# A layer kernel with RG-LRU and RWKV-7 heads: the substitution in the diagonal blocks moved from VectorE to GpSimd

## The chip, the cores and the metric

The kernel runs on one core of one Trainium2 chip. The core has five engines that run their own instruction queues in order and wait for each other by semaphores: PE (TensorE, matrix products), DVE (VectorE), ACT (ScalarE), POOL (GpSimd) and SP (SyncE, which issues the DMAs here). The metric is the device time of one execution in microseconds; lower is better.

## The reference, cut to what matters

The reference is one decoder layer in float32 over 512 tokens of 2048 features: an adaLN-modulated mixing sub-layer whose heads are half RG-LRU and half RWKV-7, then a SwiGLU sub-layer and a final norm. The change concerns the recurrence of the RWKV-7 heads (16 heads of 64 features):

```python
def step(state, inp):
    r_t, d_t, k_t, v_t, kk_t, a_t = inp
    sa = jnp.einsum('bhvk,bhk->bhv', state, -kk_t)
    state = (state * d_t[:, :, None, :]
             + sa[..., None] * (kk_t * a_t)[:, :, None, :]
             + v_t[..., None] * k_t[:, :, None, :])
    y_t = jnp.einsum('bhvk,bhk->bhv', state, r_t)
    return state, y_t
...
_, y = lax.scan(step, s0, xs)
```

## The kernel before

Large products are done as three float32r products of operands that are split exactly in two: `load_split` (L112) loads a weight tile of 128x512, ACT writes its high part (`whi`, L105) and DVE the rest (`wlo`, L106), and `mm3` (L122) issues `hi*hi`, `lo*hi` and `hi*lo` at L124, L125 and L126. Three buffers hold such split tiles.

The RWKV heads are worked in 8 pairs of heads, the 512 tokens in 8 chunks of 64. Within a chunk the recurrence is a triangular system, so each chunk needs the inverse of a 64x64 unit triangular matrix for each head. `rwkv_half` (L596) prepares four chunks of a pair (a "half"): among others the products `ps_gr` of L633, their masked copy `rw_gb` (L635) and, packed from its diagonal 32-blocks, `rw_dg` (L637, L639). It ends with `inverse` (L750 on), which is called 16 times, once for each half of each pair:

- L757, DVE: a 32x32 transpose spreads the diagonal blocks, one to a partition, as `rw_at`; L760 sets `rw_x` to the identity.
- L764 and L766: the forward substitution. 31 steps, each a product of two operands into `rw_xp` and an addition to `rw_x`, every one of them needing the one before; an instruction covers all 128 partitions and from 4 to 46 elements of each.
- L768 and L771, DVE: two transposes give the inverted blocks as `rw_xn` and `rw_xs`. L775, POOL: four copies into `bd_xt`.
- L783 and L793, PE: the lower left blocks from `rw_xn` and `rw_xs`; then the chain of the pair's state (`rwkv_chain`, L666) may use the half.

`rwkv_weave` runs five streams of such steps side by side: the chains, the first halves, the second halves, `rwkv_main` (what a pair needs of all tokens), and columns of the adaLN modulation (L199, `adaq`). Where none of them can go on, `weave` (L145) takes a step of the filler: the input projections, the RG-LRU heads (whose `lru_gates` has a one-column memset on POOL at L885, read by DVE at L887), and half of the output projection. `weave` decides by planned latencies, for an inverse `INVLAT = 30.2` us, in which order the steps are written. From that, the scheduler of the framework makes the order of each engine's queue, and inserts the semaphores. On POOL stand, beside the copies of L775, two copies for each half (L616, `bd_a`) and one memset for each pair (L554).

Of the kernel before, what the change touches and what calls it, by code (L numbers as in the profile page):

```python
# [8 lines left out]
F32 = mybir.dt.float32  # L9
# [3 lines left out]
ALU = mybir.AluOpType  # L13
AX = mybir.AxisListType
PSUM = bass.MemoryType.PSUM
DRAM = bass.MemoryType.DRAM

P = 128
S = 512
# [7 lines left out]
C = 64  # L27
# [6 lines left out]
# latencies (us) that weave() goes by when it orders steps; they bear on the order only  # L34
HOP = 1.10                      # a small product, its copy out of PSUM
LM1, LM2, LM3 = 4.2, 6.8, 9.0   # the steps of rwkv_main
LH0 = 4.8                       # rwkv_half's operands
INVLAT = 30.2                   # substitution in the diagonal blocks
LSN = 1.79                      # the next state
MODLAT = (4.0, 3.8, 2.0)        # a quarter of a column of mod, by kind  # L40

# columns of the packed per-feature vectors (one column holds 128 features)
# [14 lines left out]
# columns of the constants (shapes alone)  # L57
# [29 lines left out]
class Layer:  # L87
# [24 lines left out]
    def load_split(self, src, n):  # L112
        """src: DRAM [128, n] -> (hi, lo) float32r tiles [128, n]"""
        raw = self.wp.tile([P, self.wc], F32, tag="raw", name="wraw", bufs=self.wb[0])
        self.nc.sync.dma_start(out=raw[:, :n], in_=src)
        hi = self.wp.tile([P, self.wc], F32R, tag="whi", name="whi", bufs=self.wb[1])
        lo = self.wp.tile([P, self.wc], F32R, tag="wlo", name="wlo", bufs=self.wb[1])
        with self.tc.high_priority():
            self.split_into(hi[:, :n], lo[:, :n], raw[:, :n])
        return hi, lo  # L120
# [7 lines left out]
    def gemm_steps(self, ps, src, acts):  # L128
        """ps[128, S] = W^T acts, src: DRAM [128, nk * 128], acts: list of (hi, lo); yields after each k"""
        nk = len(acts)  # L130
        kp = self.wc // P
        for k0 in range(0, nk, kp):
            kn = min(kp, nk - k0)
            hi, lo = self.load_split(src[:, k0 * P:(k0 + kn) * P], kn * P)
            for k in range(kn):
                sl = slice(k * P, (k + 1) * P)
                self.mm3(ps, (hi[:, sl], lo[:, sl]), acts[k0 + k], k0 + k == 0, k0 + k == nk - 1)
                yield
# [6 lines left out]
    def weave(self, streams, filler):  # L145
        """Traces the next step of the first stream that can run, a step of filler when none can.
        A stream yields (its last step's us on the tensor engine, the us until the next can run,
        what must hold in the trace before that); filler yields None or such a condition."""
        t = 0.0
        live = [[g, 0.0, None] for g in streams]  # L150
        fcond = None
        while live:
            for st in live:
                if st[1] <= t and (st[2] is None or st[2]()):
                    try:
                        with self.tc.issue_after(self.pe):
                            dur, lat, st[2] = next(st[0])
                        t += dur
                        st[1] = t + lat
                    except StopIteration:  # L160
                        live.remove(st)
                    break
            else:
                if filler is not None and (fcond is None or fcond()):
                    try:
                        fcond = next(filler)
                        t += 0.65
                    except StopIteration:
                        filler = None
                else:  # L170
                    t = min(st[1] for st in live if st[2] is None or st[2]())

# [1 line left out]
    def mod_pair(self, j):  # L174
        """columns j and j + 16"""
        nc = self.nc
        part = self.small.tile([P, 2], F32, tag="adapart", name="adapart", bufs=2)
        for h in range(2):
            t = self.ada.tile([P, D], F32, tag="ada", name="ada", bufs=4)
            nc.sync.dma_start(out=t, in_=self.i["w_ada"][j + 16 * h])  # L180
            nc.vector.scalar_tensor_tensor(out=t, in0=t, scalar=1.0, in1=self.cbc, op0=ALU.mult,
                                           op1=ALU.mult, accum_out=part[:, h:h + 1])
        o = _VOFF["b_ada"] + j
        nc.vector.tensor_tensor(out=self.mod[:, j:j + 17:16], in0=part, in1=self.vecs[:, o:o + 17:16],
                                op=ALU.add)

    def mod_steps(self, js, pool, tags):
        """the same for many columns, a quarter of c at a time"""
# [22 lines left out]
    def mod_scale(self, col, sc, g):  # L211
        """col = g * (1 + mod[:, sc])"""
        self.nc.vector.scalar_tensor_tensor(
            out=col, in0=self.mod[:, sc:sc + 1], scalar=1.0, in1=g, op0=ALU.add, op1=ALU.mult)

    def square(self, acc, x, k, pool):
        """acc += x * x"""
        if k == 0:
            self.nc.scalar.activation(out=acc, in_=x, func=AF.Square)
        else:  # L220
            t = pool.tile([P, S], F32, tag="ft", name="sqt", bufs=2)
            self.nc.scalar.activation(out=t, in_=x, func=AF.Square)
            self.nc.vector.tensor_tensor(out=acc, in0=acc, in1=t, op=ALU.add)

    def norm(self, acc, tag):
        """1 / rms of each token, in all partitions (PSUM), from sums of squares by partition"""
# [16 lines left out]
    def modulate(self, x, col, rstd, sh, lo=None):  # L243
        """hi, lo of x * col * rstd + sh"""
# [54 lines left out]
    def mixing(self):  # L299
# [3 lines left out]
        with ExitStack() as ctx:  # L303
            self.open_ada(ctx)
            with tc.tile_pool(name="xs", bufs=1) as xs:
# [16 lines left out]
                # seven tiles stay in PSUM, four more take turns in the last bank by quarters of K  # L322
# [43 lines left out]
    def rwkv_weave(self, kvr0, kvr1, u0):  # L366
# [16 lines left out]
        def filler():  # L383
# [15 lines left out]
            # half of the channels through the output projection  # L399
# [45 lines left out]
    def project(self, ys, half, *tags):  # L445
        """x1 += g_m * (ys through their half of w_out)"""
# [29 lines left out]
    def rwkv_setup(self, ctx):  # L476
# [4 lines left out]
        # zero at the first token of each chunk  # L481
# [3 lines left out]
        # block-diagonal operands (two heads); what lies off the blocks stays zero  # L485
# [7 lines left out]
    def lora_act(self, m, ps, pool):  # L493
        """what the second products of the low ranks take, the parts of a float32 stacked by rows:
        tanh(w) (hi, lo), a (lo, hi), all of g's first 128 rows, the other 32 (-, hi, lo, hi)"""
# [26 lines left out]
    def rwkv_main(self, pr):  # L522
        """what a pair of heads needs of all the tokens"""
# [16 lines left out]
        # decay and its running product within a chunk  # L540
# [21 lines left out]
        # kk = k * k_k over its norm per head  # L562
# [15 lines left out]
        # k' = k (1 + (a - 1) k_a), the bonus, v by tokens  # L578
# [17 lines left out]
    def rwkv_half(self, pr, hf):  # L596
        """four chunks of a pair"""
# [21 lines left out]
        # v by tokens, centred over its features  # L619
# [9 lines left out]
        # products within the chunks  # L629
# [36 lines left out]
    def rwkv_chain(self, pr):  # L666
        """a pair's state through the chunks, its output"""
# [9 lines left out]
        # through the chunks  # L677
# [49 lines left out]
        # group norm (y is centred already), bonus, gate  # L727
# [22 lines left out]
    def inverse(self, hf, dg, gb):  # L750
        """bd["xt"][hf]: the transposed inverse of I - A of each head and chunk, A^T in gb[:, :, :C]"""
# [3 lines left out]
        # diagonal 32-blocks, one to a partition (eight partitions share its columns)  # L755
# [6 lines left out]
        for s in range(31):  # L762
            n, j = 31 - s, s // 8 + 1
            tt(out=pr[:, :n, :j], in0=at[:, s + 1:, s:s + 1].to_broadcast([P, n, j]),  # L764
               in1=x[:, s:s + 1, :j].to_broadcast([P, n, j]), op=ALU.mult)
            tt(out=x[:, s + 1:, :j], in0=x[:, s + 1:, :j], in1=pr[:, :n, :j], op=ALU.add)  # L766
        xn = rw.tile([P, 32, 4], F32, tag=f"at{hf}", name="rw_xn")      # [t, j, chunk]
        nc.vector.transpose(out=xn.rearrange("p (j r) c -> p j (r c)", r=8),  # L768
                            in_=x.rearrange("p t j -> p j t"))
        xs = rw.tile([P, 4, 32], F32, tag=f"dg{hf}", name="rw_xs")      # [j, chunk, t]  # L770
# [7 lines left out]
        # lower left blocks: X21 = X22 A21 X11  # L778
# [22 lines left out]
    def lru_setup(self, ctx):  # L801
# [3 lines left out]
        # softplus(-lam) = max(-lam, 0) + 2 atanh(e / (2 + e)), e = exp(-|lam|)  # L805
# [24 lines left out]
    def lru_conv(self, j, pss=None):  # L830
        """head j: convolution"""
# [23 lines left out]
    def lru_gates(self, j):  # L855
        """gates, scan"""
# [18 lines left out]
        for m in range(2):  # L875
# [6 lines left out]
            # 1 - a^2 = tanh(-log a) (1 + a^2)  # L882
# [7 lines left out]
    def lru_gelu(self, j, pool, tags):  # L890
        """head j: its gelu branch"""
# [8 lines left out]
    def lru_out(self, j):  # L900
        """head j's product"""
# [78 lines left out]
def _tiles(w, mt=None):  # L980
    """[K, M] -> [M / 128, 128, K]: column tile m, partition p (row k * 128 + p), free (k, column)"""
# [4 lines left out]
def _pack(inp):  # L986
# [17 lines left out]
    lw = np.stack([a["lru_wa"][0], a["lru_wx"][0]], axis=1)          # [4, 2, 256, 256]  # L1004
# [41 lines left out]
```

## Time and profile before

| | |
|---|---|
| time, median of 3 runs | 2511.34 us (2509.75 to 2511.64) |
| the profiled execution: span from first to last instruction | 2515.8 us; the page gives no other time of it |
| busy: PE, DVE, ACT, POOL | 96%, 55%, 34%, 3% of the span |
| the weave of the RWKV heads | about 200 to 930 us of the span |
| L764 and L766 | 496 instructions each, 224.4 to 881.7 us |

The page's slices show in which part DVE is loaded; each digit is the busy share of a fortieth of the span (63 us) in tenths, PEclk the clock that PE was granted.

```profile
PE   5999999999999999899999999999999999999997
DVE  7979898999969847854423322233322233222244
POOL 0000111111101000000000000000000000000000
PEclk9999998999999999999999999999999999999998
```

DVE is near 9 tenths from the fourth to the fourteenth slice, which is the weave, and at 2 to 4 tenths in the SwiGLU part behind it. The first number behind a group in the tables of groups is its busy time in us, the second the mean time of one instruction in ns, and what follows the bar is the idle time of the engine ahead of it.

### The profile page before, as it was taken

What the parts mean: (1) busy time and instruction counts of PE and PEld (TensorE: products, weight loads), DVE (VectorE), ACT (ScalarE), POOL (GpSimd) and SP (SyncE); (2) the same over time, 40 slices, a digit from 0 to 9 for tenths busy, and PEclk for the clock granted to TensorE, in tenths of its full rate; (3) what the DMA queues carried; (4) which work ended last, traced back from release to release, by engine and by line L of the source; (5) the groups of instructions that cost most, each with busy time, mean ns of one, the idle gap of its engine ahead of it and who ended that gap; (6) DMA issues with size and microseconds to landing.
All of it is one profiled execution on the core that took longest, in us unless ns stands there. A gap on an engine that the chain in (4) does not pass through costs nothing.

```text
span 2515.8 us, 30983 instructions
## 1 busy us (share of the span) xinstructions
PE 2413.9 (96%) x11560; PEld 1953.4 (78%) x11560; DVE 1380.4 (55%) x3111; ACT 843.7 (34%) x1340; POOL 82.0 (3%) x131
## 2 busy tenths in 40 slices
PE   5999999999999999899999999999999999999997
PEld 3677777877777886687788888888888888888885
DVE  7979898999969847854423322233322233222244
ACT  4357364455355333432222222222222222222221
POOL 0000111111101000000000000000000000000000
PEclk9999998999999999999999999999999999999998
DMA  8864444444342438366423332323333233333233
GB/s 304 308 219 130 148 128 143 131 152 144 125 135 81 143 108 283 119 195 194 160 90 95 108 100 93 101 83 98 106 98 99 89 92 105 101 93 100 85 95 112
DMA packets 138938, 333.22 MB, mean 132 GB/s; under 512 B 15458, under 2 KB 28898, under 8 KB 134690
## 3 DMA queue, kind: packets, MB, share of 16 engines
q1 hardware_dynamic: 138788, 331.25, 40.7%
q8 instruction: 90, 1.47, 0.2%
q14 instruction: 60, 0.49, 0.1%
HBM read 322.92 MB, written 7.87 MB: 131 GB/s over the span
## 4 chain that ended last, share of the span: by engine, by line
PE 72%; DVE 9%; DMA 7%; issue 1%; ACT 1%; SPq 0%; POOL 0%; DVEq 0%; ACTq 0%
PE ps_mm L124 10%; PE ps_mm L126 10%; PE ps_mm L125 10%; PE ps_gr L126 6%; PE ps_st L124 6%; PE ps_gr L124 6%; PE ps_st L126 6%; PE ps_gr L125 6%; PE ps_st L125 6%; DMA adaq<-in_w_ada 6%; DVE adaq L199 2%; DVE wlo L106 2%; DVE rw_xp L764 1%; DVE rw_x L766 1%; DMA wraw<-in_w_out 1%
## 5 line engine op out<-in xcount | busy, mean ns | idle before, releaser
L106 DVE TENSOR_TENSOR wlo<-wraw,whi 128x1024 fp32r<-128x1024 f32 (+2 forms) x552 | 496.7, 902 | 730.2 <-ACT whi L105 721.1
L105 ACT CAST whi<-wraw 128x1024 fp32r<-128x1024 f32 (+2 forms) x552 | 436.6, 792 | 1292.4 <-PE ps_mm L125 401.1
L124 PE MATMUL ps_mm<-hhi,whi 128*128 128x512 f32 x1020 | 417.1, 410 | 9.8 <-ACT hhi L251 7.2
L126 PE MATMUL ps_mm<-hhi,wlo 128*128 128x512 f32 x1020 | 407.2, 399 | 1.7 <-DVE wlo L106 1.6
L125 PE MATMUL ps_mm<-hlo,whi 128*128 128x512 f32 x1020 | 406.5, 399 | 0.8 <-DVE hlo L252 0.7
L124 PEld LDWEIGHTS ps_mm<-hhi,whi 128*128 128x128 f32 x1020 | 193.4, 190 | 53.2 <-ACT hhi L251 9.9
L125 PEld LDWEIGHTS ps_mm<-hlo,whi 128*128 128x128 f32 x1020 | 193.7, 190 | 43.4 <-DVE hlo L252 4.8
L126 PEld LDWEIGHTS ps_mm<-hhi,wlo 128*128 128x128 f32 x1020 | 193.8, 190 | 42.3 <-DVE wlo L106 3.0
L199 DVE SCALAR_TENSOR_TENSOR adaq<-adaq,cbq 128x512 f32<-128x512 f32 x256 | 173.5, 687 | 92.9 <-DMA adaq<-in_w_ada 85.1
L126 PE MATMUL ps_gr<-hhi,wlo 128*128 128x512 f32 x496 | 193.7, 390 | 3.1 <-DVE wlo L106 3.1
L126 PE MATMUL ps_st<-hhi,wlo 128*128 128x512 f32 x496 | 193.6, 390 | 2.0 <-DVE wlo L106 2.0
L124 PE MATMUL ps_st<-hhi,whi 128*128 128x512 f32 x496 | 194.0, 391 | 1.6 <-ACT hhi L251 1.6
L125 PE MATMUL ps_gr<-hlo,whi 128*128 128x512 f32 x496 | 193.5, 390 | 0.0
L125 PE MATMUL ps_st<-hlo,whi 128*128 128x512 f32 x496 | 193.5, 390 | 0.0
L124 PE MATMUL ps_gr<-hhi,whi 128*128 128x512 f32 x496 | 192.6, 391 | 0.0
L126 PEld LDWEIGHTS ps_gr<-hhi,wlo 128*128 128x128 f32 x496 | 93.4, 188 | 23.6 <-DVE wlo L106 4.1
L126 PEld LDWEIGHTS ps_st<-hhi,wlo 128*128 128x128 f32 x496 | 93.4, 188 | 21.8 <-DVE wlo L106 2.5
L124 PEld LDWEIGHTS ps_st<-hhi,whi 128*128 128x128 f32 x496 | 93.5, 188 | 21.6 <-ACT hhi L251 2.2
L125 PEld LDWEIGHTS ps_gr<-hlo,whi 128*128 128x128 f32 x496 | 93.7, 189 | 19.6
L124 PEld LDWEIGHTS ps_gr<-hhi,whi 128*128 128x128 f32 x496 | 93.7, 189 | 19.4
L125 PEld LDWEIGHTS ps_st<-hlo,whi 128*128 128x128 f32 x496 | 93.3, 188 | 19.8 <-DVE hlo L252 0.3
L766 DVE TENSOR_TENSOR rw_x<-rw_x,rw_xp 128x27 f32<-128x27 f32 (+23 forms) x496 | 94.7, 196 | 5.7
(312 smaller groups left out, 3809.6 us busy)
## 6 DMA issues: line engine op xcount, KB each, us to landing
wraw<-in_w_gu SPq DMA_DIRECT2D x176, 512.0 KB, 3.6
adaq<-in_w_ada SPq DMA_DIRECT2D x256, 256.0 KB, 3.3
wraw<-in_w_in SPq DMA_DIRECT2D x160, 256.0 KB, 3.0
ada<-in_w_ada SPq DMA_DIRECT2D x32, 1024.0 KB, 7.2
wraw<-in_w_down SPq DMA_DIRECT2D x64, 512.0 KB, 3.5
wraw<-in_w_out SPq DMA_DIRECT2D x64, 256.0 KB, 3.3
wraw<-in_w_down SPq DMA_DIRECT2D x64, 192.0 KB, 2.3
x<-in_x SPq DMA_DIRECT2D x32, 256.0 KB, 5.3
```

The costliest lines, as they stand in the source:

```text
L105: nc.scalar.copy(out=hi, in_=src)
L106: nc.vector.tensor_tensor(out=lo, in0=src, in1=hi.bitcast(F32), op=ALU.subtract)
L124: mm(ps, lhsT=w[0], rhs=x[0], start=start, stop=False)
L125: mm(ps, lhsT=w[0], rhs=x[1], start=False, stop=False)
L126: self.pe = mm(ps, lhsT=w[1], rhs=x[0], start=False, stop=stop).ins
L199: nc.vector.scalar_tensor_tensor(out=t, in0=t, scalar=1.0, in1=cb, op0=ALU.mult, op1=ALU.mult, accum_out=part[:, m, h:h + 1])
L764: tt(out=pr[:, :n, :j], in0=at[:, s + 1:, s:s + 1].to_broadcast([P, n, j]), in1=x[:, s:s + 1, :j].to_broadcast([P, n, j]), op=ALU.mult)
L766: tt(out=x[:, s + 1:, :j], in0=x[:, s + 1:, :j], in1=pr[:, :n, :j], op=ALU.add)
```

## The change

The two instructions of each substitution step are issued on GpSimd instead of VectorE, in all 16 calls of `inverse`. Comments are emptied as well, line for line; the one added line shifts what stands behind it by one: L757, L764, L766, L768, L771, L775, L783, L793, L885, L887 are L758, L765, L767, L769, L772, L776, L784, L794, L886, L888 afterwards. The planned latencies stay as they are.

```diff
@@ -748,11 +748,12 @@
     def inverse(self, hf, dg, gb):
...
         nc, rw = self.nc, self.rw
         mm = nc.tensor.matmul
         tt = nc.vector.tensor_tensor
-        # diagonal 32-blocks, one to a partition (eight partitions share its columns)
+        gt = nc.gpsimd.tensor_tensor
+
         at = rw.tile([P, 32, 32], F32, tag=f"at{hf}", name="rw_at")
@@ -761,13 +762,13 @@
         pr = rw.tile([P, 31, 4], F32, tag=f"dg{hf}", name="rw_xp")
         for s in range(31):
             n, j = 31 - s, s // 8 + 1
-            tt(out=pr[:, :n, :j], in0=at[:, s + 1:, s:s + 1].to_broadcast([P, n, j]),
+            gt(out=pr[:, :n, :j], in0=at[:, s + 1:, s:s + 1].to_broadcast([P, n, j]),
                in1=x[:, s:s + 1, :j].to_broadcast([P, n, j]), op=ALU.mult)
-            tt(out=x[:, s + 1:, :j], in0=x[:, s + 1:, :j], in1=pr[:, :n, :j], op=ALU.add)
+            gt(out=x[:, s + 1:, :j], in0=x[:, s + 1:, :j], in1=pr[:, :n, :j], op=ALU.add)
```

The orders of the queues change with it. POOL's queue before, from the memset of the second pair on, where the copies of the first two inverses (`bd_xt`) and of the next half (`bd_a`) follow each other:

```order
L554 MEMSET rw_pb 128x8 [waits DVE_49,Activation_49,Pool_49]
L885 MEMSET lru_ulo 128x1 [waits PE_49,Activation_49] x2
L775 TENSOR_SCALAR bd_xt_1406<-rw_xs 32x4x32 [waits DVE_49]
L775 TENSOR_SCALAR bd_xt_1406<-rw_xs 32x4x32 [waits Pool_49]
L775 TENSOR_SCALAR bd_xt_1406<-rw_xs 32x4x32 x2
L616 TENSOR_SCALAR bd_a_1394<-rw_ar 64x4x64 [waits DVE_49,Pool_49]
```

POOL's queue now, at the end of the first inverse and the start of the second:

```order
L765 TENSOR_TENSOR rw_xp<-rw_at,rw_x 128x4 [waits Pool_49]
L767 TENSOR_TENSOR rw_x<-rw_x,rw_xp 128x4 [waits Pool_49]
L886 MEMSET lru_ulo 128x1 [waits PE_49,Activation_49]
L776 TENSOR_SCALAR bd_xt_1406<-rw_xs 32x4x32 [waits DVE_49]
L776 TENSOR_SCALAR bd_xt_1406<-rw_xs 32x4x32 [waits Pool_49]
L776 TENSOR_SCALAR bd_xt_1406<-rw_xs 32x4x32 x2
L765 TENSOR_TENSOR rw_xp<-rw_at,rw_x 128x31 [waits DVE_49,Pool_49]
L767 TENSOR_TENSOR rw_x<-rw_x,rw_xp 128x31 [waits Pool_49]
L765 TENSOR_TENSOR rw_xp<-rw_at,rw_x 128x30 [waits Pool_49]
```

The 62 instructions of an inverse now stand between the copies, each with a wait for POOL's own semaphore; the first memset of `lru_ulo` stands among those of the first inverse, the second at its end.

DVE's queue now, 19 instructions behind the transpose (L758) that starts the first inverse; `wlo_2125` and `wlo_2175` are parts of split weights for PE:

```order
L888 TENSOR_TENSOR lru_g1_1846<-lru_g1_1846,lru_ulo_1870 128x512 [waits Pool_49]
L884 SCALAR_TENSOR_TENSOR lru_ulo_1881<-lru_g0_1858,lru_ulo_1881 128x512 [waits Activation_49]
L106 TENSOR_TENSOR wlo_2125<-wraw_2122,whi_2124 128x512 [waits DMAHW6_49,PE_49,Activation_49]
L769 STREAM_TRANSPOSE rw_xn_1826<-rw_x_1761 128x128 [waits Pool_49]
L889 SCALAR_TENSOR_TENSOR lru_g0_1746<-lru_uhi_1869,lru_g1_1846 128x512 [waits DVE_49]
L772 STREAM_TRANSPOSE rw_xs_1828<-rw_xn_1826 128x128 [waits DVE_49]
L906 TENSOR_TENSOR lru_g0_1746<-lru_g0_1746,lru_ge_1590 128x512 [waits DVE_49]
L758 STREAM_TRANSPOSE rw_at_1973<-rw_dg_1929 128x1024
L199 SCALAR_TENSOR_TENSOR adaq_2202,adaparts_1448<-adaq_2202,cbq_1449 128x512 [waits DMAHW7_49]
L887 TENSOR_TENSOR lru_g1_1867<-lru_g1_1867,lru_u_1463 128x512 [waits Activation_49]
L106 TENSOR_TENSOR wlo_2175<-wraw_2172,whi_2174 128x512 [waits DMAHW0_49,PE_49,Activation_49]
```

Before, the same transpose (L768) waited for DVE alone and had some 160 instructions between it and L757, the 62 of its own substitution among them. Now it waits for POOL, and the transpose that starts the second inverse stands behind it.

PE's queue now, where the first product reads `wlo_2175`, and then 38 rows later, where the first inverse is read:

```order
L126 MATMUL ps_mm_2121<-hhi_392,wlo_2125 128x512
L124 MATMUL ps_mm_2121<-hhi_520,whi_2174 128x512
L125 MATMUL ps_mm_2121<-hlo_521,whi_2174 128x512
L126 MATMUL ps_mm_2121<-hhi_520,wlo_2175 128x512
L124 MATMUL ps_mm_2121<-hhi_570,whi_2174 128x512
```

```order
L124 MATMUL ps_mm_2246<-hhi_248,whi_2249 128x512
L125 MATMUL ps_mm_2246<-hlo_249,whi_2249 128x512
L126 MATMUL ps_mm_2246<-hhi_248,wlo_2250 128x512
L784 MATMUL ps_gr_2256<-rw_xn_1826,rw_gb_1701 32x32 x8
L124 MATMUL ps_mm_2246<-hhi_296,whi_2249 128x512
```

The L633 of this inverse stands 86 rows ahead of the first of these two places; L784 stood 205 rows behind it before, and stands 124 rows behind it now.

## The prediction

> **What bounds the kernel now.** I read the page's first lines, then the busy time in stretches of the span, then the waits of PE, then the groups of DVE and POOL.
>
> ```profile
> span 2515.8 us, 30983 instructions
> PE 2413.9 (96%) x11560; PEld 1953.4 (78%) x11560; DVE 1380.4 (55%) x3111; ACT 843.7 (34%) x1340; POOL 82.0 (3%) x131
> core 0: us, PE busy (x) PEld busy (x) DVE busy (x) ACT busy (x) POOL busy (x), PEclk, DMA share, GB/s
> 200.00:300.00 100.00, 95.59 (x551) 74.34 (x550) 93.17 (x294) 55.58 (x101) 11.76 (x17) 0.98 0.42 133
> 300.00:400.00 100.00, 94.01 (x539) 75.63 (x538) 86.46 (x277) 52.62 (x102) 9.15 (x15) 0.93 0.40 123
> 400.00:500.00 100.00, 96.17 (x559) 76.37 (x559) 89.61 (x304) 48.53 (x95) 12.18 (x16) 0.95 0.45 143
> 500.00:600.00 100.00, 95.99 (x572) 75.91 (x571) 93.50 (x307) 55.12 (x105) 9.27 (x15) 0.98 0.48 151
> 600.00:700.00 100.00, 94.42 (x597) 76.72 (x596) 88.81 (x308) 45.48 (x97) 12.21 (x17) 0.95 0.44 137
> 700.00:800.00 100.00, 93.73 (x506) 73.25 (x504) 81.04 (x280) 59.37 (x102) 9.10 (x15) 0.97 0.31 98
> 800.00:900.00 100.00, 100.00 (x662) 82.68 (x661) 77.58 (x232) 40.52 (x97) 12.36 (x17) 1.00 0.38 123
> ```
>
> The change lies in 200 to 900 us. PE is the bound there: it is busy 670 of 700 us, so 30 us are idle, and the clock column, averaged, loses another 24 us (the seven shares fall short of 1 by 0.24 in all). DVE is at 78 to 93%, POOL at about 11%. PE's waits say what the idle time is:
>
> ```profile
> PE ps_gr L783 <- DVE rw_xn L768: 18.7, 8, 3.7
> PE ps_st L568 <- ACT rw_t L566: 2.5, 2, 2.2
> PE ps_mm L124 <- DVE mix_r L472: 2.3, 1, 2.3
> ```
>
> Of the 30 us, 18.7 are eight waits for the inverse that the change moves. These eight and the two single waits of over 2 us below them are what I count as ten gaps; 24 us of lost clock over ten gaps makes **2.4 us of half clock per gap**. That the two belong together is seen around one of them:
>
> ```profile
> 600.00:602.70 2.70, 0.64 (x3) 0.19 (x1) 2.57 (x13) 2.66 (x5) 0.00 (x0) 1.00 0.73 238
> 603.00:606.60 3.60, 3.60 (x26) 3.21 (x21) 3.38 (x7) 3.14 (x6) 2.77 (x4) 0.53 0.67 203
> ```
>
> PE idles 2.06 of 2.7 us, and then runs at 0.53 of its clock. The Trainium skill (TensorE: Matmul & The Clock Gate, Part 1) lets the clock fall only after an idle window of about 3.4 us and come back after as long a busy one, so a long wait would cost 1.7 us instead of 2.4 (an estimate from that page), and the sum below would be 16 x 0.7 = 11 us less by it. This trace disagrees on the first half: about 2 us idle were enough.
>
> **What is removed.** The 992 small operations of DVE:
>
> ```profile
> L106 DVE TENSOR_TENSOR wlo<-wraw,whi 128x512 fp32r<-128x512 f32 x145 | 99.4, 686 | 12.6 <-ACT whi L105 9.8 <-PE ps_mm L126 0.9 <-issue 0.4
> L766 DVE TENSOR_TENSOR rw_x<-rw_x,rw_xp 128x27 f32<-128x27 f32 (+23 forms) x496 | 94.7, 196 | 5.7
> L764 DVE TENSOR_TENSOR rw_xp<-rw_at,rw_x 128x27 f32<-128x27 f32 (+23 forms) x496 | 94.2, 195 | 6.0
> ```
>
> That is 94.7 + 94.2 = 189 us of DVE busy time. DVE is not the bound, so the 189 us by themselves buy nothing; they buy at most the waits for the inverse, 18.7 us and their share of the half clock. With all ten gaps' clock counted in, the most that can be won is 19 + 24 = **43 us**.
>
> **What is added: the price t of one substitution step on POOL.** No row shows a two-operand operation on POOL. The nearest are its copies and its memset:
>
> ```profile
> L775 POOL TENSOR_SCALAR bd_xt<-rw_xs x64: 517/527/1017, 275.1 to 885.0; 32x128 f32<-32x128 f32 x64
> L775 POOL TENSOR_SCALAR bd_xt<-rw_xs 32x128 f32<-32x128 f32 x64 | 39.9, 623 | 287.2 <-DVE rw_xs L771 142.1 <-DVE rw_xp L764 123.9 <-DVE rw_x L766 17.8
> L616 POOL TENSOR_SCALAR bd_a<-rw_ar x32: 844/990/1830, 213.4 to 849.4; 64x256 f32<-64x256 f32 x32
> L554 POOL MEMSET rw_pb<- 128x8 f32 x8 | 0.9, 113 | 0.4
> 670.37 1.91 POOL L616 TENSOR_SCALAR bd_a<-rw_ar 64x256 f32<-64x256 f32 x2 [12.32 <-DVE rw_x L766]
> 672.34 0.11 POOL L554 MEMSET rw_pb<- 128x8 f32 x1
> 433.79 0.41 DVE L771 STREAM_TRANSPOSE rw_xs<-rw_xn 128x128 f32<-128x128 f32 x1
> 434.19 0.68 DVE L199 SCALAR_TENSOR_TENSOR adaq<-adaq,cbq 128x512 f32<-128x512 f32 x1
> 434.28 3.06 POOL L775 TENSOR_SCALAR bd_xt<-rw_xs 32x128 f32<-32x128 f32 x4 [21.09 <-DVE rw_xp L764]
> ```
>
> Least copy times 517 ns at 128 elements and 844 ns at 256 give 2.55 ns per element and 190 ns without any. The 31 steps have 920 elements, so 30 per operation: 190 + 77 = 267 ns. A second operand that is read one after the other adds at most another 77 ns: 0.27 to 0.34, of which I take 0.30. Every operation waits for a semaphore of the one before it. The one such place here is the memset, which starts at 672.34, 0.06 us after the copies end at 672.28; a wait across engines takes 0.08 (transpose done at 434.20, copy starts at 434.28). I take 0.08. Last, interference: that copy of 434.28 starts beside a two-operand DVE instruction, and its four take 3.06 us where four at 527 ns and three gaps of 0.06 to 0.08 would take 2.3. So DVE delays POOL by some 0.25 us per meeting. Between starting an inverse and stopping for it (below) DVE has about 6.6 us of work, some ten such instructions: 2.5 us per inverse, 0.04 per operation. **t = 0.30 + 0.08 + 0.04 = 0.42 us**, 26.0 us per inverse of 62. Bounds: 0.33 with the least of each (0.27 + 0.06), and from far above 0.70, the 128-element copy's mean of 623 ns with its gap of 0.08.
>
> **Where it stands on the path.** The substitution used to be mixed into DVE's queue; now L769, the transpose of its result, is one DVE instruction that waits for POOL, and the order puts it only 6 to 19 instructions behind L758, which starts the inverse. What is queued behind it are the L106 splits, without which PE has no weights. So PE does not stop at L784: it stops at the first product that reads a split from behind L769. I count PE's time from L633, which begins the inverse, to that product in the new order: in the sixteen inverses 54 to 89 big products and some small ones. A big one costs 0.23 us:
>
> ```profile
> 268.06 0.39 PE L125 MATMUL ps_mm<-hlo,whi 128*128 128x512 f32 x1
> 268.29 0.39 PE L126 MATMUL ps_mm<-hhi,wlo 128*128 128x512 f32 x1
> 268.51 0.39 PE L124 MATMUL ps_mm<-hhi,whi 128*128 128x512 f32 x1
> 283.96 0.38 PE L696 MATMUL ps_ch<-rw_s,bd_a 128*128 128x128 f32 x2
> 284.18 0.33 PE L712 MATMUL ps_y<-rw_ar,rw_s 128*128 128x64 f32 x2
> ```
>
> With 0.22 us for a small float32 product (283.96 to 284.18) and the others by their own spacing, this gives 20.3 to 26.7 us, in the mean **23.6 us** (67 big products are 15.4 of it). Against it stands what the inverse needs:
>
> ```profile
> 474.81 1.16 PE L633 MATMUL ps_gr<-rw_ar,bd_b 128*128 128x128 f32 x8
> 479.32 2.03 DVE L757 STREAM_TRANSPOSE rw_at<-rw_dg 128x1024 f32<-128x1024 f32 x1
> ```
>
> 4.5 us from L633 to the first transpose, 2.0 for it, 0.1 to reach POOL, 26.0 for the substitution, and 2.8 from there through L769 and what DVE has queued ahead of the first split behind it (from one to nine instructions; 2.6 in the mean with 0.6 per big one, and 0.2 of hops): 35.4 us. **PE waits 35.4 - 23.6 = 11.8 us for each of 16 inverses, 189 us.** In pairs 0 and 6 both halves start 7 to 8 us apart; POOL does them one after the other, and the second waits some 9 us more: +18. Sixteen gaps of half clock at 2.4: +38. The old gaps go: -43. POOL's other work (copies of L616, L776, the memsets) queues behind the substitution, but in the order it stands between two inverses; what waits for it, above all DVE's L888, stops together with L769, and I cost it at nothing more; with that cover gone it would be a few us per head of the LRU, of which there are four. The DMAs do not move past anything.
>
> Sum: 189 + 18 + 38 - 43 = **+202 us**. The profiled execution's span of 2515.8 (the page gives nothing around it) lies 4.5 above the median of the timed runs, so I carry the difference over: 2511.3 + 202 = **2713 us**.
>
> **The rivals.**
>
> Faster: POOL's small operation costs little more than its memset, 0.11 + 0.08 = 0.19. From 0.23 down (62 t below 23.6 - 9.4) the result is there before the first blocked split; PE never waits, the 43 us go, and 2511 - 43 gives 2468. The memset's row speaks for it, both copies' rows, which start from 190 ns, against it. 0.05.
>
> The stop of DVE is harmless, because PE has splits enough in store, and PE waits at L784 alone: that lies some 37 us behind L633 for most inverses, over the 33.4 that are then needed (35.4 less the 2.0 of DVE's queue). Only four fall short (one of each crowded pair by 17 and 20, two more by 13 and 7): 57 + 10 of half clock - 43 = +24, 2535. The three buffers of the splits speak for it, the order, in which they are already used up, against it. 0.05.
>
> A second operand costs POOL a second start. Copy against memset, 190 ns without elements against 113 with eight, says that reading one operand costs some 75 ns; a second would make t 0.49 to 0.50. Then 62 t = 30.4, the wait 16.2 us, and 259 + 18 + 38 - 43 = +272: 2783. The Trainium skill states such a thing (GPSIMD Engine Reference, section 7): a read command costs about 102 cycles that do not overlap with the one before. No run here shows two operands. 0.22. Above that (t of 0.55 gives 34.1, a wait of 19.9, +331: 2842) 0.10.
>
> **How the numbers follow.** My forecast, with t from its lower bound of 0.33 (29.9 us needed, a wait of 6.3, 101 + 18 + 38 - 43 = +114, 2625) to about 0.47, has 0.58. The range is 2590 to 2830: it leaves out the first two rivals and half of the last, 0.15, and a little below 2625 is taken in because the crowded pairs cost less than 18 at a small t. A difference of 0.2% (5 us) is about what a measurement of this kernel can tell from no change; faster 0.05 (the first rival), same 0.02 (of the second, with t at its lower bound), slower 0.93 (all the rest).
>
> **What would show it.** POOL gets 992 operations of about 0.30 us that start 0.42 us apart, and its busy time goes from 82 to some 380 us. DVE's waits are led by L769 for POOL, 16 times about 19 us. PE waits for wlo of L106 (at L124 to L126), some 200 us in all, and hardly at L784; the clock stays below 1. Wrong would be: PE's wait named L784 (then the splits were in store), or a step of POOL outside 0.33 to 0.55.

## The result, and the profile after

The changed kernel takes 2710.89 us (median of 4 runs, 2708.83 to 2712.64), the kernel before 2510.55 us on the same chip (2509.55 to 2511.64): a ratio of 1.0794, with a 95% interval from 1.0779 to 1.0809. It is slower, by 200 us; 2713 was forecast.

The first lines of the page:

```profile
span 2710.3 us, 31089 instructions
PE 2429.5 (90%) x11560; PEld 1967.6 (73%) x11560; DVE 1255.2 (46%) x2119; ACT 843.4 (31%) x1339; POOL 376.9 (14%) x1123
```

DVE's busy time fell by 125 us, and PE, which sets the time, is busy for 90% of the span where it was for 96%. PE's busy time for the same 11560 products grew by 15.6 us (2413.9 to 2429.5); the granted clock of the two executions is 0.986 before and 0.955 after in the mean, and I take the growth to be that. PE's idle time is the span less its busy time, 101.9 us before and 280.8 after. So the 194.5 us between the two spans are 178.9 us of new idle time on PE and 15.6 of longer products.

PE's waits from 200 to 1150 us (in all, times, longest), with those under 5 us left out:

```profile
PE ps_ch L696 <- DVE rw_s L720: 108.6, 12, 16.1
PE ps_mm L124 <- DVE mix_r L472: 17.7, 3, 16.5
PE ps_mm L126 <- DVE wlo L106: 16.4, 2, 11.1
PE ps_ch L701 <- POOL bd_xt L776: 15.0, 1, 15.0
PE ps_st L655 <- ACT rw_bn L657: 14.0, 1, 14.0
PE ps_mm L124 <- DVE mix_v L472: 12.9, 1, 12.9
PE ps_ch L696 <- DVE rw_s L722: 10.5, 1, 10.5
PE ps_gr L784 <- DVE rw_xn L769: 8.6, 1, 8.6
```

They sum to 203.7 us. The 16 longest waits among them are one for each of the sixteen inverses, 199.8 us together and 12.5 in the mean. Only the last row names the inverse. The other names look harmless, and all but one (L655, of which more below) are an instruction that stands in DVE's queue behind the stopped transpose, or wait for one that does. What stops DVE and how long, and how long GpSimd's two kinds of operations take:

```profile
DVE rw_xn L769 <- POOL rw_x L767: 221.4, 15, 16.1
DVE lru_g L888 <- POOL lru_ulo L886: 20.8, 5, 13.2
...
L767 POOL TENSOR_TENSOR rw_x<-rw_x,rw_xp 128x24 f32<-128x24 f32 (+23 forms) x496 | 155.5, 314 | 38.0
L765 POOL TENSOR_TENSOR rw_xp<-rw_at,rw_x 128x24 f32<-128x24 f32 (+23 forms) x496 | 140.1, 283 | 160.8 <-DVE rw_at L758 123.9
```

One of the sixteen stops, in order of time (start, duration, engine and line; in brackets the idle time before it and what ended it):

```profile
455.74 0.29 POOL L767 TENSOR_TENSOR rw_x<-rw_x,rw_xp 128x45 f32<-128x45 f32 x1
...
464.60 0.20 POOL L767 TENSOR_TENSOR rw_x<-rw_x,rw_xp 128x4 f32<-128x4 f32 x1
464.83 0.40 DVE L769 STREAM_TRANSPOSE rw_xn<-rw_x 128x128 f32<-128x128 f32 x1 [15.23 <-POOL rw_x L767]
465.16 0.65 DVE L106 TENSOR_TENSOR wlo<-wraw,whi 128x512 fp32r<-128x512 f32 x1
...
466.73 0.33 SPq L195 DMA_DIRECT2D cbq<-csilu  x1
...
467.10 0.69 DVE L106 TENSOR_TENSOR wlo<-wraw,whi 128x512 fp32r<-128x512 f32 x1
...
471.07 0.69 DVE L199 SCALAR_TENSOR_TENSOR adaq<-adaq,cbq 128x512 f32<-128x512 f32 x1 [3.28 <-DMA cbq<-csilu]
471.69 0.08 DVE L199 DVE_READ_ACCUMULATOR adaq<-adaq,cbq 128x1 f32 x1
471.69 0.35 DVE L720 SCALAR_TENSOR_TENSOR rw_s<-ps_ch,rw_pcs,rw_w 128x128 f32<-128x128 f32 x1
472.09 0.50 PEld L696 LDWEIGHTS ps_ch<-rw_s,bd_a 128*128 128x128 f32 x2 [16.31 <-DVE rw_s L720]
472.09 0.80 PE L696 MATMUL ps_ch<-rw_s,bd_a 128*128 128x128 f32 x2 [16.12 <-DVE rw_s L720]
```

DVE stands for 15.23 us at L769. PE, out of work since 456.0 us, does not need L769's result. It needs the next state of the chain, L720, a product of 0.35 us whose operands are long there. It starts 6.9 us after DVE goes on, because seven instructions stand between the two in DVE's queue, and the last of them waits 3.28 us for a load that was itself issued only at 466.73, after DVE had gone on.

### The profile page after: what moved, and what is told of

It reads as the page before. It is cut to its first block, busy times and chain, and to the rows that moved or that the text cites. A ratio compares the mean times of both kernels' runs of the same rounds, so it can differ in the third digit from the quotient of the medians.

```text
span 2710.3 us, 31089 instructions
## 1 busy us (share of the span) xinstructions
PE 2429.5 (90%) x11560; PEld 1967.6 (73%) x11560; DVE 1255.2 (46%) x2119; ACT 843.4 (31%) x1339; POOL 376.9 (14%) x1123
## 4 chain that ended last, share of the span: by engine, by line
PE 55%; DMA 6%; DVE 3%; POOL 3%; issue 1%; ACT 1%; SPq 0%; DVEq 0%; ACTq 0%; POOLq 0%
PE ps_mm L124 7%; PE ps_mm L126 7%; PE ps_mm L125 7%; PE ps_st L126 5%; PE ps_gr L124 5%; PE ps_gr L125 5%; PE ps_st L124 5%; PE ps_st L125 5%; PE ps_gr L126 5%; DMA adaq<-in_w_ada 4%; POOL rw_x L767 1%; DMA wraw<-in_w_out 1%; POOL rw_xp L765 1%; DVE adaq L199 1%; DVE wlo L106 1%
## 5 line engine op out<-in xcount | busy, mean ns | idle before, releaser
L106 DVE TENSOR_TENSOR wlo<-wraw,whi 128x1024 fp32r<-128x1024 f32 (+2 forms) x552 | 498.4, 905 | 756.9 <-ACT whi L105 743.5
L124 PE MATMUL ps_mm<-hhi,whi 128*128 128x512 f32 x1020 | 426.8, 420 | 21.2 <-DVE mix_v L472 12.9
L126 PE MATMUL ps_mm<-hhi,wlo 128*128 128x512 f32 x1020 | 409.0, 401 | 17.5 <-DVE wlo L106 17.4
L124 PEld LDWEIGHTS ps_mm<-hhi,whi 128*128 128x128 f32 x1020 | 197.2, 194 | 64.2 <-issue 17.3
L126 PEld LDWEIGHTS ps_mm<-hhi,wlo 128*128 128x128 f32 x1020 | 197.1, 193 | 61.8 <-DVE wlo L106 19.5
L124 PE MATMUL ps_st<-hhi,whi 128*128 128x512 f32 x496 | 194.0, 391 | 1.6 <-ACT hhi L251 1.6
L126 PE MATMUL ps_st<-hhi,wlo 128*128 128x512 f32 x496 | 193.7, 390 | 1.4 <-DVE wlo L106 1.4
L126 PE MATMUL ps_gr<-hhi,wlo 128*128 128x512 f32 x496 | 193.3, 390 | 1.1 <-DVE wlo L106 1.1
L124 PE MATMUL ps_gr<-hhi,whi 128*128 128x512 f32 x496 | 192.6, 391 | 0.0
L765 POOL TENSOR_TENSOR rw_xp<-rw_at,rw_x 128x24 f32<-128x24 f32 (+23 forms) x496 | 140.1, 283 | 160.8 <-DVE rw_at L758 123.9
L767 POOL TENSOR_TENSOR rw_x<-rw_x,rw_xp 128x24 f32<-128x24 f32 (+23 forms) x496 | 155.5, 314 | 38.0
L696 PE MATMUL ps_ch<-rw_s,bd_a 128*128 128x128 f32 x112 | 26.2, 320 | 119.2 <-DVE rw_s L720 108.6
L769 DVE STREAM_TRANSPOSE rw_xn<-rw_x 128x128 f32<-128x128 f32 x16 | 6.4, 403 | 223.2 <-POOL rw_x L767 221.4
L696 PEld LDWEIGHTS ps_ch<-rw_s,bd_a 128*128 128x128 f32 x112 | 19.4, 212 | 123.9 <-DVE rw_s L720 111.5
L124 PEld LDWEIGHTS ps_st<-hhi,whi 128*128 128x128 f32 x496 | 93.5, 188 | 21.6 <-ACT hhi L251 2.2
L126 PEld LDWEIGHTS ps_st<-hhi,wlo 128*128 128x128 f32 x496 | 93.4, 188 | 21.5 <-DVE wlo L106 2.3
```

What stands on the lines that cost most here:

```text
L106: nc.vector.tensor_tensor(out=lo, in0=src, in1=hi.bitcast(F32), op=ALU.subtract)
L124: mm(ps, lhsT=w[0], rhs=x[0], start=start, stop=False)
L126: self.pe = mm(ps, lhsT=w[1], rhs=x[0], start=False, stop=stop).ins
L696: mm(ps, lhsT=ba, rhs=sbd, start=False, stop=True)
L765: gt(out=pr[:, :n, :j], in0=at[:, s + 1:, s:s + 1].to_broadcast([P, n, j]), in1=x[:, s:s + 1, :j].to_broadcast([P, n, j]), op=ALU.mult)
L767: gt(out=x[:, s + 1:, :j], in0=x[:, s + 1:, :j], in1=pr[:, :n, :j], op=ALU.add)
```

## The experiments

Three theories were set against each other. **Stop:** the loss is an engine that stands in its queue for GpSimd while others need what is queued behind. **Rival 1:** GpSimd is too slow for the recurrence itself, wherever the wait stands. **Rival 2:** GpSimd's work slows DVE and ACT beside it. All runs, with the kernel before at 2508.6 to 2512.1 us beside them:

| run | what is different | median us | ratio to before, interval |
|---|---|---|---|
| e1_late | transposes later | 2575.1 | 1.0268 (1.0247 to 1.0290) |
| e2_late_dve | the same, substitution on DVE | 2518.5 | 1.0038 (1.0025 to 1.0052) |
| e3_mid | transposes less late | 2648.5 | 1.0551 (1.0529 to 1.0572) |
| e4_unread | result unread | 2568.3 | 1.0235 (1.0217 to 1.0253) |
| e5_late_memset | e1, memset on DVE | 2566.5 | 1.0222 (1.0197 to 1.0247) |
| e6_unread_free | e4, two waits less, one new | 2699.7 | 1.0752 (1.0721 to 1.0784) |
| e7_half | second halves on GpSimd alone | 2571.6 | 1.0235 (1.0206 to 1.0264) |
| e8_late_memset_later | e5, first product later | 2571.2 | 1.0239 (1.0212 to 1.0266) |
| e9_unread_nostop | e6, new wait removed | 2490.1 | 0.9917 (0.9897 to 0.9936) |
| e10_half_split | e7, first halves' transposes at their old place, their copies on DVE | 2548.1 | 1.0146 (1.0128 to 1.0163) |
| e11_more | 31 operations more per inverse | 2817.9 | 1.1215 (1.1189 to 1.1240) |
| e12_late34 | e5, transposes later still | 2562.2 | 1.0198 (1.0174 to 1.0221) |

### GpSimd's work without the stop

In e4_unread the 992 operations run at their place, but their result is left out: the transposes read the constant start matrix. They write into the buffer of `rw_at`, so the multiplications read another part of it (not shown in the cut):

```diff
-        xn = rw.tile([P, 32, 4], F32, tag=f"at{hf}", name="rw_xn")
+        xn = flat[:, 0:128].rearrange("p (t c) -> p t c", c=4)
...
-                            in_=x.rearrange("p t j -> p j t"))
+                            in_=self.con("xinit").rearrange("p (t j) -> p j t", j=4))
```

> GpSimd runs all 992 operations at the same place, beside the same work, but its result is not used: the transposes read the constant start matrix, so DVE waits for nothing, and the output lacks the substitution. Theory: no stop, no loss, and the 43 us of old gaps go too: 2468 us, between 2455 and 2495. Rival 2 (GpSimd's operations slow DVE beside them, through the memory they share): 2560 us or more, and the mean of DVE's two-operand instructions is above the 686 ns of the split before. Rival 1 says nothing of this run.

Measured: 2568.3 us, 143 below the change, but 100 above what the theory said. The number fits rival 2, and so does its second sign: the mean of DVE's split rose from 686 to 710 ns (L106, 128x512, from 200 to 900 us). But this run still has waits for GpSimd:

```profile
DVE lru_g L890 <- POOL lru_ulo L888: 43.8, 7, 17.1
...
ACT rw_rt L790 <- POOL rw_x L769: 32.6, 5, 11.6
...
DVE rw_x L761 <- POOL rw_xp L767: 9.0, 1, 9.0
```

The one-column memset of the LRU stood in GpSimd's queue behind a substitution, and ACT copied into the buffer that GpSimd worked in. e6_unread_free takes these two away:

```diff
-            nc.gpsimd.memset(th[:, 0:1], 1.0)
+            nc.vector.memset(th[:, 0:1], 1.0)
...
-        rt = rw.tile([P, 4, 32], F32, tag=f"x{hf}", name="rw_rt")
+        rt = flat[:, 256:384].rearrange("p (c t) -> p c t", t=32)
```

> e4_unread without its two remaining waits for GpSimd: the memset of the LRU goes to DVE, and the buffer into which ACT copies the first product of the inverse is no longer the one that GpSimd works in. GpSimd still runs all 992 operations beside the same work; the result is still not used. Theory (all of the loss is engines that wait for GpSimd, in one queue or another): 2475 us, between 2460 and 2495. Rival 2 (GpSimd's operations slow the engines beside them): it stays at 2540 or more.

Measured: 2699.7 us, 131 us worse. The theory is missed by far; rival 2's "2540 or more" holds by number, but gives no reason for a loss where two waits were taken away. The DVE waits show one:

```profile
DVE rw_x L761 <- POOL rw_x L769: 225.1, 14, 19.1
```

Now that ACT no longer used that buffer, the scheduler put the next pair's copy of the start matrix (L761) into DVE's queue as soon as it thought the buffer free, and there it waited for the running substitution. That is the wait of the change again, at another line, for a buffer and not for a result. e9_unread_nostop differs from e6 in this one copy:

```diff
-        nc.vector.tensor_copy(out=x.rearrange("p t j -> p (t j)"), in_=self.con("xinit"))
+        nc.gpsimd.tensor_copy(out=x.rearrange("p t j -> p (t j)"), in_=self.con("xinit"))
```

> e6_unread_free without the wait that its trace shows in place of the old one: there DVE's copy of the start matrix for the next pair (L761) stood some 60 us too early in DVE's queue and waited 14 times, 225 us in all, for GpSimd to leave that buffer. Here GpSimd copies its start matrix itself; DVE and ACT wait for no substitution. GpSimd still runs all 992 operations, with the result not used. Theory (all of the loss is an engine that stops in its queue for GpSimd): 2480 us, between 2460 and 2505. Rival 2 (GpSimd's operations slow the engines beside them, whoever waits): 2540 or more.

Measured: 2490.1 us, as the theory said, and 20 us below the kernel before. Its page, and GpSimd's groups:

```profile
span 2488.7 us, 31080 instructions
PE 2393.7 (96%) x11560; PEld 1941.9 (78%) x11560; DVE 1257.1 (51%) x2111; ACT 843.0 (34%) x1339; POOL 466.2 (19%) x1131
...
L769 POOL TENSOR_TENSOR rw_x<-rw_x,rw_xp 128x24 f32<-128x24 f32 (+23 forms) x496 | 195.3, 394 | 37.4
L767 POOL TENSOR_TENSOR rw_xp<-rw_at,rw_x 128x24 f32<-128x24 f32 (+23 forms) x496 | 184.2, 372 | 81.8 <-DVE rw_at L758 44.5
```

No wait of DVE for GpSimd is left, and GpSimd is busier than in any other run with 992 operations. So rival 2 falls: DVE's splits are as long as in e4 (709 ns), and the kernel is faster than before all the same. Against 2468 us, which the prediction's 43 us would leave, GpSimd's work beside the others costs some 22 us at most. Between e6 and e9 lie one copy, 225 us of DVE's waits and 210 us of the kernel. So DVE's stops at one place of its queue, 14 of 16 us each, are worth as much as the whole loss of the change (200 us), shown by a single edit. Both runs leave the result unread; what the stop is worth where the result is used, the next runs show.

### The same result, asked for later

e1_late keeps the result in use. The step with the two transposes is traced 30.2 us later and put behind a split of weights (`issue_after` holds it there in DVE's queue):

```diff
+        yield 0, INVLAT, None
+        with self.tc.issue_after(self.lo):
             xn = rw.tile([P, 32, 4], F32, tag=f"at{hf}", name="rw_xn")
...
-        yield 0, INVLAT, None
+        yield 0, 1.5, None
```

e2_late_dve is the same with the substitution on DVE, and e3_mid has `yield 0, 23, None` in place of the first line and `yield 0, 7.2, None` in place of the last.

> The substitution stays on GpSimd. The step that holds the two transposes of the result is traced 30.2 us later and put behind the split of weights traced last, so that the first product that needs anything queued behind the stopped transpose on DVE lies 31 to 53 us of PE work behind the start of its inverse (mean 38.8) instead of 16 to 26 (mean 21.6); about 33 us are needed by the trace of the change. Theory (DVE's stop in the middle of its queue is the whole loss): the waits go but for the second inverse of the two crowded pairs (some 20 us), and with them the waits of the kernel before: 2511 - 43 + 20 = 2490 us, between 2465 and 2520. Rival 1 (GpSimd is too slow for the recurrence itself; PE would wait for the inverse at its first product in any order): 2650 us or more. Rival 2 (GpSimd's 314 us of small operations slow DVE and ACT beside them): 2600 us or more, with longer DVE instructions.

> Control for the placing alone: the same later transposes, with the substitution on DVE as before. Theory: nothing of weight, 2511 us within 15, since no DVE instruction waits for another engine there. If the placing by itself were worth much, this would be far below 2511, and e1_late would have to be read against it.

> As e1_late, but the step with the transposes is traced 23 us behind the start of its inverse and not 30.2. By the order the first blocked product then lies 22 to 35 us of PE work behind the start (mean 28.4). Theory (wait = what is needed, 33 us, less that distance, for each of the 16): 76 us of waits and some 18 in the crowded pairs, 2511 - 43 + 94 + 15 to 25 of half clock = about 2580 us, between 2550 and 2630. Rival 1 and rival 2: about as after the change, 2680 to 2710, since GpSimd does the same work.

Measured: 2575.1, 2518.5 and 2648.5 us. The control moves by 0.4%, so placing alone is worth little. With the substitution on GpSimd the order of the three is the theory's: the later DVE stops, the less it costs, from 2711 over 2649 to 2575, with the same work on GpSimd. Rival 1 falls with that, as far as it explains the 200 us. The sizes are not the theory's: e1 is 85 us and e3 68 us above the expected value, both outside the range that was given. Part of the reason is in GpSimd's groups of e1:

```profile
L767 POOL TENSOR_TENSOR rw_x<-rw_x,rw_xp 128x24 f32<-128x24 f32 (+23 forms) x496 | 179.1, 361 | 38.6
L765 POOL TENSOR_TENSOR rw_xp<-rw_at,rw_x 128x24 f32<-128x24 f32 (+23 forms) x496 | 175.1, 353 | 145.4 <-DVE rw_at L758 97.1 <-ACT rw_kn L657 10.6
...
DVE rw_xn L771 <- POOL rw_x L767: 63.6, 11, 12.6
```

Operations of 314 and 283 ns became ones of 361 and 353. One substitution takes 23.3 us in the change, 25.3 in e3 and 27.2 in e1 (means of 16, first operation to last). A DVE that stops less holds GpSimd up more, so the 33 us that I took as needed grew by up to 4.

### The waits that were left

```diff
-            nc.gpsimd.memset(th[:, 0:1], 1.0)
+            nc.vector.memset(th[:, 0:1], 1.0)
```

is the edit of e5_late_memset against e1. e8_late_memset_later has `yield 0, 3.0, None` behind the transposes too.

> e1_late with one more edit: the one-column memset of the LRU (before DVE's multiply of the gate) goes from GpSimd to DVE, so it no longer stands in GpSimd's queue behind a substitution. Theory (in e1_late GpSimd's queue is the second way in which the substitution stops DVE: 31.9 us of DVE's waits are for that memset, and PE stands for 14.0 and 8.5 us in two of them): those two gaps go, with some half clock, 2575 - 25 = 2550 us, between 2538 and 2560. Rival (those gaps only hide another wait that ends as late, or GpSimd's operations slow the rest): 2565 to 2580.

> e5_late_memset with the first product of the inverse traced 3.0 us behind the transposes instead of 1.5. In e1_late PE waited 12.6 us at that product. Theory: these go, 2550 - 13 = 2537 us, between 2515 and 2550; what is left is the crowded pairs. Rival: no difference to e5_late_memset (within 6 us).

Measured: 2566.5 and 2571.2 us. Of the 25 us expected of the memset 8.6 came, with intervals that touch (1.0247 is the low end of e1 and the high end of e5). The rival had it right: PE's wait of 14.0 us in the first pair went, and a little later in the same pair its wait at L701 grew from 5.7 to 11.6 us (first row), where the load of the inverse's block matrix waited 12.1 us for GpSimd (second row):

```profile
PE ps_ch L701 <- ACT rw_w L698: 17.0, 3, 11.6
...
PEld ps_ch L701 <- POOL bd_xt L778: 19.8, 2, 12.1
```

e8's further delay bought nothing, though DVE's waits at the transpose fell from 95.9 us in e5 to 54.2: what was left of DVE's stops was no longer what PE waited for. Two versions kept the first half of each pair on DVE; e7_half has `gt = (nc.gpsimd if hf else nc.vector).tensor_tensor` on top of e8, and e10_half_split leaves the first half's transposes at their place and copies its blocks on DVE (`ce = nc.gpsimd if hf else nc.vector`).

> A version meant to gain: e5_late_memset with the substitution of the first half of each pair on DVE as before and that of the second half on GpSimd, and the first product of the inverse traced 3.0 us behind the transposes instead of 1.5. Theory: no two substitutions on GpSimd at once, half of DVE's relief is left, no stop that PE reaches; 2500 us, between 2470 and 2520, so at or a little below the kernel before (2509). Rival 2 (slowing by GpSimd): 2530 or more.

> A version meant to gain: the first half of each pair is left as before (substitution on DVE, transposes where they were) and its copies into the block matrix go to DVE too, so that they do not stand in GpSimd's queue behind the second half's substitution, as they did in e7_half (11.9 us of PE in one wait); the second half's substitution is on GpSimd with its transposes later, and the memset of the LRU is on DVE. Theory: no queue is stopped by GpSimd where PE needs it; 2500 us, between 2475 and 2520. Rival 2: 2530 or more.

Measured: 2571.6 and 2548.1 us. In e7 the first half's copies stood in GpSimd's queue behind the second half's substitution, and PE waited 11.9 us at L701 in one pair; with e10's two edits 23 us went, but it is still 1.5% above before. e12_late34 is e5 with the transposes traced 34 us behind the start, 50 for the second half of the crowded pairs (0 and 6), and put behind a split of a weight, no other:

> A version meant to gain, from what the traces show of the need: with DVE free beside it a substitution takes 27 to 31 us on GpSimd and not 23, so that 38 to 41 us are needed and not 33. All substitutions on GpSimd, the memset of the LRU on DVE, the transposes traced 34 us behind the start (50 us for the second half of the two crowded pairs) and behind the split of a weight. By the order the first blocked product is then 43.5 us of PE work behind the start in the mean (four of the sixteen below 40). Theory: what is left is a few waits of some us; 2505 us, between 2490 and 2525, against 2510 before and 2490 for e9_unread_nostop, in which nothing waits. If placing is not what is left of e5_late_memset's loss, it stays at 2550 or more.

Measured: 2562.2 us, 57 us above the expected value. DVE now waits for the substitutions for 26.0 us in all (221.4 in the change), so the stop is gone for most, and of the 200 us of the change 149 came back with the result in use. PE's waits from 200 to 1000 us, longest sums first, have no leader:

```profile
PE ps_ch L701 <- POOL bd_xt L782: 15.1, 2, 11.2
PE ps_mm L124 <- ACT yhi L105: 9.5, 2, 8.9
PE ps_ch L696 <- DVE rw_s L720: 8.1, 5, 3.2
PE ps_gr L790 <- DVE rw_gb L635: 6.5, 2, 5.2
```

PE is busy 2424.5 us there and 2393.7 in e9, for the same products, and the mean granted clock is 0.976 and 0.993: 31 of the 79 us between the two profiled executions are longer products, the rest is PE's idle time. What makes these short waits is not settled. The six versions that use the result and were placed for it (e1, e5, e7, e8, e10, e12) stay 38 to 67 us above the kernel before; how much of that is the longer substitution itself, a small rival 1, stays open. With nothing waiting for GpSimd there were 20 us to be had, and no version that uses the result came near it.

### More operations

```diff
+            gt(out=pr[:, :n, :j], in0=at[:, s + 1:, s:s + 1].to_broadcast([P, n, j]),
+               in1=x[:, s:s + 1, :j].to_broadcast([P, n, j]), op=ALU.mult)
```

> The change with each of the 31 multiplications of a substitution run twice (496 more operations on GpSimd, the same result). By the order the first product behind the stopped transpose moves from 21.6 to 25.5 us of PE work behind the start of its inverse, in the mean. Theory (PE's wait is what the inverse needs less that distance; an operation costs 0.378 us from start to start in the trace of the change): 31 x 0.378 = 11.7 us more are needed, 3.9 less of it counts, 7.8 x 16 = 125, and twice 11.7 in the crowded pairs, so 2711 + 148 = about 2860 us, between 2820 and 2895. If GpSimd's pace did not matter (the stop costs a fixed sum for each of the 16), 2711 within 20.

Measured: 2817.9 us, 107 above the change where 148 were expected.

```profile
DVE rw_xn L771 <- POOL rw_x L769: 331.3, 16, 24.7
```

GpSimd's pace matters, since DVE's stops grew from 221.4 to 331.3 us. The 31 operations cost 10.0 us per inverse and not 11.7 (33.3 against 23.3 us from first to last). That is 0.32 us each, about what the timeline above has while DVE stands still, and with it the theory gives (10.0 - 3.9) x 16 + 2 x 10.0 = 118 us; the last 11 are not placed.

## Why the prediction was right

**Removed work buys nothing by itself: right.** DVE's busy time fell by 125 us, and no time came of it. (It fell by less than the 189 that were removed, because the records of the small operations overlapped those of their neighbours: without them DVE is busy 1272 us before and 1255 after.) The most that could be won was put at 43 us; e9, in which nothing waits, wins 20.

**t, the price of a step: body right, spacing too dear.** 0.30 us was forecast for an operation, the two groups above have 0.298 in the mean; from start to start 0.42 was forecast and 0.378 is measured, 23.3 us per inverse and not 26.0. The term for interference was worked out for a DVE that runs; in the change DVE stands still for most of the substitution. With DVE hardly held up (e9) the spacing is 0.509 us. The rival with a second start for the second operand (0.49) does not hold: beside no DVE instruction, an operation takes 0.20 to 0.29 us, as the timeline's rows for 45 and for 4 elements have it, less than a copy of 128.

**DVE stops at L769: right.** 15 stops of 14.8 us in the mean (16 of 19 were forecast). Of the 4.2 us 2.7 are the cheaper steps; the rest is, by the difference, a DVE that comes to L769 later than I had counted.

**What PE waits for: the step that failed.** "PE waits for wlo of L106 (at L124 to L126), some 200 us in all" was written; that row has 16.4 us. The first thing that PE needs from behind the stop is mostly the chain's next state, L720: 108.6 us in all, where eight of the twelve waits are the long one of an inverse. I had counted only the splits. Counting every DVE result behind L769 in the same way in the order, the first needed one lies 21.6 us of PE work behind L633, in the mean, not 23.6. By itself this would have raised the waits by 2.0 x 16 = 32 us; the cheaper steps took 2.7 x 16 = 43 off.

**The sum:** 189 + 18 us of waits were forecast for sixteen inverses; the eight rows above have 203.7 in all. The +18 for the crowding of pairs 0 and 6 did not come: their four waits are 14.0 (L655) and 11.1 us (L126), 12.9 (mix_v) and 5.3 (L126), 10.8 in the mean, and those of the other twelve inverses 13.0. In pair 0 the two substitutions were not even side by side: the transpose that starts the second stood in DVE's queue behind the first one's stop, and began 2.3 us after the first substitution had ended. With the three sizes put right the sum would be 189 + 32 - 43 = 178 us; the other 26 are not placed. So the forecast of the time came out as close as it did (2713 for 2711) partly by luck, through errors of opposite sign; that DVE stops and that PE then stands for about 12 us per inverse was foreseen. **The clock:** 38 - 24 = +14 us was forecast net, PE's busy time grew by 15.6.

**What was costed at nothing:** "DVE's L888, stops together with L769" was true in effect. In the first inverse L888 took the place of L769: DVE stood 13.2 us there and 1.8 at L769, and PE's wait of 14.0 us (L655) ended with a chain that began at that memset. That this made the sum larger is not shown. e4 shows what this cover was worth once L769 no longer stopped: 43.8 us of DVE's time.

**The rivals.** PE hardly waits at L784 (8.6 us), so the stop of DVE was not harmless. How long the splits in store would have lasted is not shown, since PE mostly stood for the chain before it came to them. A cheap operation of 0.19 us did not come.

## What to carry to other kernels

When work moves from one in-order engine to a slower one, look first for the one instruction that stays behind and waits for it, then list everything that is queued behind that instruction, whatever its size, and find which of it the bounding engine needs first. Taking load off an engine that is not the bound buys little; one wait in its queue that is placed too early can cost the whole length of the moved work, and so can a buffer's reuse or a one-column memset that lands behind it. Check the queue of the receiving engine as well: everything small that it did before now stands behind 20 to 30 us.

## What was not expected of the hardware

GpSimd is held by DVE much more than DVE by GpSimd. From e9, where both run (start, duration):

```profile
324.18 0.73 DVE L886 SCALAR_TENSOR_TENSOR lru_ulo<-lru_g,lru_ulo 128x512 f32<-128x512 f32 x1
324.44 0.59 POOL L769 TENSOR_TENSOR rw_x<-rw_x,rw_xp 128x36 f32<-128x36 f32 x1
...
326.42 0.25 POOL L769 TENSOR_TENSOR rw_x<-rw_x,rw_xp 128x30 f32<-128x30 f32 x1
...
328.11 0.69 DVE L635 TENSOR_TENSOR rw_gb<-ps_gr,cons 128x512 f32<-128x512 f32 x1
...
328.35 0.23 POOL L767 TENSOR_TENSOR rw_xp<-rw_at,rw_x 128x28 f32<-128x28 f32 x1
...
330.01 1.25 DVE L891 TENSOR_TENSOR_SCAN lru_g<-lru_uhi,lru_g 128x512 f32<-128x512 f32 x1
330.26 1.02 POOL L767 TENSOR_TENSOR rw_xp<-rw_at,rw_x 128x20 f32<-128x20 f32 x1
```

With no DVE instruction beside it, an operation takes 0.25 us. Beside a DVE instruction with two operands in SBUF (L886) it takes 0.59 and ends 0.12 us behind that instruction; beside a scan (L891, also two operands in SBUF) 1.02, again until its end. Beside L635, which reads one operand from PSUM, it takes 0.23, as if alone. The other way round, DVE's splits (L106, 128x512) went from 686 ns before to 709 in e9. The Trainium skill (SBUF — State Buffer, "SBUF: two separate sides") says that a GpSimd instruction that reads SBUF and a DVE instruction with two inputs in SBUF take turns at a shared pair of ports, each for a whole instruction. The trace agrees (0.59 and 1.02 us until the DVE instruction's end, 0.23 beside L635). It shows one consequence in numbers: the many short operations pay (0.378 us from start to start in the change, where DVE stands for most of the substitution, 0.509 in e9, where it runs), the few long ones hardly do, and freeing DVE from a wait makes the thing it waited for slower.
